# Conditioning columns loaded and multiplied later, one weight split ahead of a branch, and lower weight halves on another engine

## The chip, the cores and the metric

One core of a Trainium2 chip runs the whole program. The metric is the device time of one execution in microseconds (us). Five engines work side by side and meet at semaphores: PE (TensorE, matmuls and transposes), DVE (VectorE), ACT (ScalarE), POOL (GpSimd) and SP (SyncE), which here only issues transfers from HBM.

## The reference, cut to what matters

Two layers over 512 tokens of width 1024. Each layer has a token mixer and a mixture of experts, both between a modulation and a layer norm:

```
c_act = silu(c)
for i in range(2):
    mod = c_act @ ada_w[i] + ada_b[i]                  # [1024] @ [1024, 6144]
    sh1, sc1, g1, sh2, sc2, g2 = split(mod, 6)
    h = x * (1 + sc1) + sh1
    y = neighbourhood_mixer(h) if i == 0 else gqa_mixer(h)
    x = layer_norm(alpha * x + (1 + g1) * y)
    h = x * (1 + sc2) + sh2
    y = hierarchical_moe(h)                            # 32 experts, top 2
    x = layer_norm(alpha * x + (1 + g2) * y)
```

`gqa_mixer` projects 1024 columns of queries and 256 each of keys and values, normalises queries and keys, rotates them and attends. All is float32; a float32 product that must stay exact is made of a higher half and a lower half of each operand (`wh`, `wl` of a weight, `hTH`, `hTL` of the activations), and three of the four products are summed.

## The kernel before, in words

The program runs through these stages: the values, projections and neighbourhood attention of layer 0 (`mixer0`, to about 295 us), its output projection and norm (to 380), its experts (to 835), the norm and a conditional branch for overflowing experts (to 862), layer 1's projections (`mixer1`, 862 to 970), its attention and norm (to 1155), its experts (to 1610) and the end.

**Modulation.** `mod` has 12 columns of 512 numbers for each layer, addressed as (layer, j). A column takes two weight tiles of 1 MB (128 x 2048, names `w<-in_ada`). In `mixer0` the function `flow` writes out 32 steps n, one per head pair and query block. Each step does filling matmuls of the projections (`fill`), a `turn` (transposes of the probabilities), a `weigh` (`po`, probabilities times values) and the scores of a later step. In some steps `adap` multiplies two columns on PE: `ADAP` names the steps. An `adap` of two columns is 32 matmuls of 32 x 512 into one PSUM tile `pt` and an addition to `mod` on DVE (L699). From step 28 on there is no projection left to fill with; `aside` then calls `step`, which splits the output projection's weights `wo` into halves on ACT, DVE and POOL. After the last step come `close(7)` (normalising the last head pair, tiles `rze`), `flush` (`pt<-dacc`), the row `pw<-mod` and the output projection's sums (`pw<-w,oH` and `oL`), for which DVE makes the gate `g` (L935).

**Weights.** All weights are loaded by SP in the order of one list (`W`). A load waits until its buffer was read for the last time, and every later load of the list stands behind it. `w<-in_gu` are the first expert weights. `wq` is a ring of four 512 KB tiles for the projection weights of layer 0; it ends with them.

**Orders.** In `mixer0` the order on PE and DVE is that of the code, in the experts that on PE; elsewhere a scheduler orders each engine. SP's order is always that of the code.

**Layer 1's projections.** `mixer1` transposes the normalised rows, scales them into `hTH` (ACT, L419) and `hTL` (DVE, L427) through `hf`, and forms the keys from the weight `kv0` in the same loop over k (names `pj`). Weights are split by `split`: `wh` on ACT (L312), `wl = w - wh` on POOL or DVE (L313). Then come the values (`kv1`), `keys()` in the middle of the first queries, and four blocks of queries `q1_0` to `q1_3`, each through `proj`, `rope` (names `t`, `kk`, `sq`, `ss`) and `queries` (`hf`). `keys()` copies the keys twice into `kd` (ACT, L796) and takes the lower half by two subtractions, one on DVE (L797) and one on POOL (L798), before transposing (`pt<-c_ident,kd`).

**End of an expert stage.** The last two blocks `down` give `h`, `hx` and from them `YH` (ACT, L1414) and `YL` (DVE, L1415); eight `unit`s sum them to rows with statistics `bs` (DVE, L1434) and copies (ACT, L1435), then a norm, the branch, and layer 1.

Of the kernel before, what the change touches and what calls it, by code (L numbers as in the profile page):

```python
# [8 lines left out]
F32 = mybir.dt.float32  # L9
# [34 lines left out]
QPOST = 2  # L44
NWQ = 4
ADAV = [(0, 6), (0, 7), (0, 8), (0, 9), (1, 0), (1, 1), (1, 2)]
ADAP = {4: [(0, 4), (0, 5)], 8: [(0, 10), (0, 11)], 12: [(1, 4), (1, 5)], 15: [(1, 6), (1, 7)], 19: [(1, 8), (1, 9)],
        23: [(1, 10), (1, 11)], 26: [(1, 3)]}
STREAM = [("qk", 1, 0)] + [("qk", n, i) for i in (1, 2) for n in range(2)] + [("vq", 0)] \
    + [("qk", n, i) for i in (3, 4, 5, 6) for n in range(2)] + [("vq", 1)] + [("qk", n, 7) for n in range(2)]  # L50
RATE = (18, 15)
# [14 lines left out]
class Trunk:  # L66
    def __init__(self, ctx, tc, a, out, dbg=None):
        self.ctx, self.tc, self.nc, self.a, self.out = ctx, tc, tc.nc, a, out
        self.dbg = dbg or {}
        self.wl = []  # L70
        self.qfree = NWQ
        self.wi = 0
        self.wt = {}
        self.wpos = {}
        self.extra, self.free, self.owed, self.nh = [], [0] * NWB, 0, None

# [5 lines left out]
    def plan(self):  # L82
        a, wl = self.a, self.wl

        def add(key, ap, dst=None):
            self.wpos[key] = len(wl)
            wl.append((key, ap, dst))

        def ada(l, *js):
            for j in js:  # L90
                for h in range(2):
                    add(("ada", l, j, h), a["ada"][l, j, h])

        def direct(key, ap, dst):
            add(key, ap, dst)

        def xs(c0, c1):
            for t in range(NT):
                direct(("x", t, c0), a["x"][t][:, c0:c1], self.X[t][:, c0:c1])

        def aq(j, c):
            add(("aq", j, c), a["adaq"][j, c])

        for n, t in self.early:
            direct(n, a[n], t)
        for g in range(4):
            aq(g // 2, g % 2)
            aq(2 + g // 2, g % 2)
            if g == 0:
                for l in range(DEPTH):  # L110
                    direct(("adab", l), a["adab"][l], self.mod[l][0:NR])
                xs(0, 256)
                add(("v", 0, 0), a["wv"][0])
                add(("qk", 0, 0), a["wqk"][0, 0])
            elif g == 1:
                xs(256, 512)
            elif g == 2:
                xs(512, 1024)
                add(("v", 0, 1), a["wv"][1])
        for n, t in self.late:  # L120
            direct(n, bcast(a[n], [P, 36]) if n[:2] == "rb" else a[n], t)
        def ask(z):
            if z[0] == "ada":
                add(z, a["ada"][z[1], z[2], z[3]])
            elif z[0] == "qk":
                add(z, a["wqk"][z[1], z[2]])
            else:
                add(z, a["wvq"][z[1]])

        none = lambda *n: None  # L130
        self.flow(ask, lambda z, ahead: chunk_dry(z, ahead), none, none, none, none, lambda z, h, k: k or ask(("ada", *z, h)),
                  lambda pair: [ask(("ada", *z, h)) for z in pair for h in range(2)], none, none)
        for l in range(DEPTH):
            if l:
                for c in range(2):
                    add(("kv", c), a["wkv1"][c])
                for c in range(4):
                    add(("q1", c), a["wq1"][c])
            for h in range(2):
                for kh in range(2):  # L140
                    add(("wo", l, h, kh), a["wo"][l, h, kh])
            for h in range(2):
                for kh in range(2):
                    add(("wl", l, h, kh), None)
            for j in range(E // 2):
                for n in range(2):
                    for kh in range(2):
                        for i in range(2):
                            add(("gu", l, 2 * j + i, n, kh), a["gu"][l, 2 * j + i, n, kh])
                for fh in range(2):  # L150
                    for i in range(2):
                        add(("dn", l, 2 * j + i, fh), a["dn"][l, 2 * j + i, fh])
            self.wend = getattr(self, "wend", []) + [len(wl)]

    def flow(self, split, chunk, scores, turn, weigh, close, adav, adap, aside, end):


        todo, made, ready = list(STREAM), [0], set()
# [32 lines left out]
        for n in range(32):  # L191
            i, b = n // 4, n % 4
            if n + 1 < 32:
                if b == 3:
                    need(("qk", 1, i + 1))
                scores(n + 1)
            rate = RATE[n >= 12]
            fill(rate // 2)
            if b == 0 and i:
                close(i - 1)  # L200
            turn(n)
            if i < len(ADAV):
                for k in range(2):
                    adav(ADAV[i], b // 2, 2 * (b % 2) + k)
            aside(n)
            fill(rate - rate // 2)
            if n in ADAP:
                adap(ADAP[n])
            if n == 16:
                need(("vq", 0))  # L210
            if n == 24:
                need(("vq", 1))
            weigh(n)
            if n == 27:
                end()
# [137 lines left out]
    def ada_cols(self, pool, mod, dst, js, tag):  # L353
# [4 lines left out]
        for n, j, one in js:  # L358
            nc.vector.tensor_scalar(dst[:, n].rearrange("p (j i) -> p j i", j=2),
                                    pc[:, :, j:j + 2].rearrange("p i j -> p j i"), one, None, op0=OP.add)  # L360

    def row(self, ps, l, j):
        return self.mm(ps, bcast(self.indc[:, j:j + 1], [P, P]), self.mod[l], True, True)

# [64 lines left out]
    def mixer0(self, oT, right):  # L429
        tc = self.tc  # L430
        with tc.tile_pool(reuse_waits="tile", name="v0", bufs=1) as vp:
# [9 lines left out]
            with tc.manual_schedule(engines={mybir.EngineType.PE, mybir.EngineType.DVE}), \  # L441
                    tc.tile_pool(reuse_waits="tile", name="n0p", bufs=2, space=PSUM) as pp:
                q0 = self.values(vp, pp, hp, hH, hL, V, V6)
                with tc.tile_pool(reuse_waits="tile", name="n0", bufs=1) as pool:
                    def done():
                        ht.__exit__(None, None, None)
                        wo.extend(self.split_wo(0, right("wh", 4)))

                    self.neighbours(pool, pp, hp, hH, hL, V, V6, oT, q0, done, lambda: wo[1]())
        return wo  # L450

    def split_wo(self, l, pool):
# [133 lines left out]
    def neighbours(self, pool, pp, hp, hH, hL, V, V6, oT, q0, done, step):  # L586
# [83 lines left out]
        def close(i):  # L670
            self.scaled(pool, pp, oT[i // 4][:, i % 4, :].rearrange("p (b q) -> p b q", b=4), po[i], rz[i])
# [17 lines left out]
        def adap(pair):  # L689
# [8 lines left out]
                                tile_position=(0, r))  # L698
            nc.vector.tensor_tensor(self.mod[l], self.mod[l], ps, op=OP.add)  # L699

        def aside(n):
            i, b = n // 4, n % 4
            if b == 1 and i and i % 2 == 0:
# [6 lines left out]
            if n >= 28:  # L710
                step()

        self.flow(split, chunk, scores, turn, weigh, close, adav, adap, aside, done)
        close(7)
        self.accs, self.accl = [(j, accs.pop((l, j))) for l, j in ADAV[6:]], 1
        self.flush(pp)

    def mixer1(self, st, qS):
# [4 lines left out]
        with tc.tile_pool(reuse_waits="tile", name="m1", bufs=1) as pool, tc.tile_pool(reuse_waits="tile", name="m1p", bufs=2, space=PSUM) as pp:  # L723
# [8 lines left out]
            hL = pool.tile([P, KD, S], F32R, name="hTL")  # L732
            c1 = pool.tile([P, 2, KD], F32, name="c1")
            self.fold_cols(c1[:, 0], c1[:, 1], self.lnc[:, 0, 2], self.lnc[:, 0, 3], self.col[1][:, 0], self.col[1][:, 1])
            w = self.W(("kv", 0))
            whl = [self.split(pool, w[:, 1024 * x:1024 * x + 1024], [P, 1024], 4, (nc.vector, None)[x]) for x in range(2)]
            acc = [pp.tile([P, 4, HD], F32, name="pj", bufs=4) for t in range(NT)]
            for k in range(KD):
                self.put_hT(k, self.transp(k, pp, "pt"), hH, hL, c1[:, 0], c1[:, 1], pool, k >= KACT)
# [2 lines left out]
                for t in range(NT):  # L742
                    ts = slice(128 * t, 128 * t + 128)
                    po = acc[t].rearrange("p h d -> p (h d)")
                    self.mm(po, hH[:, k, ts], wh[:, c], k == 0, False)
                    self.mm(po, hH[:, k, ts], wl[:, c], False, False)
                    self.mm(po, hL[:, k, ts], wh[:, c], False, k == KD - 1)

            def proj(key):
                w = self.W(key)  # L750
                hl = [self.split(pool, w[:, 1024 * x:1024 * x + 1024], [P, 1024], 4) for x in range(2)]
                for t in range(NT):
                    ts = slice(128 * t, 128 * t + 128)
                    ps = pp.tile([P, 4, HD], F32, name="pj", bufs=4)
# [35 lines left out]
            def keys():  # L790
                r = root(ks.rearrange("p a b -> p (a b)"), 1.0, NT, "rs")
                for t in range(NT):
                    nc.vector.tensor_tensor(kk[t], kk[t], bcast(r[:, t, :, None], [P, 4, HD]), op=OP.mult)
                    kd = pool.tile([P, 2, 4, 2, HD], F32R, name="kd", bufs=1)
                    for d in range(2):
                        nc.scalar.activation(kd[:, 0, :, d, :], kk[t], AF.Copy)  # L796
                    nc.vector.tensor_tensor(kd[:, 1, :, 0, :], kk[t], kd[:, 0, :, 0, :].bitcast(F32), op=OP.subtract)  # L797
                    nc.gpsimd.tensor_tensor(kd[:, 1, :, 1, :], kk[t], kd[:, 0, :, 1, :].bitcast(F32), op=OP.subtract)  # L798
                    for n in range(2):
                        pt = pp.tile([P, 4, P], F32, name="pt")  # L800
                        for h in range(4):
# [477 lines left out]
    def moe(self, l, zH, zL, G2, rt, OH):  # L1279
        nc, X, tc = self.nc, self.X, self.tc  # L1280
        NQ = E // 4
        with tc.tile_pool(reuse_waits="tile", name=f"mo{l}", bufs=2) as pool, \
# [167 lines left out]
            for q in range(NQ):  # L1450
# [38 lines left out]
                    seed(range(NSEED[0]))  # L1489
                down(b, hx)  # L1490
            seed(range(NSEED[0], 8))
            for n in range(8):
                unit(n)
            self.scales(pool, rt, 0, NT)
# [142 lines left out]
```

## Time and profile before

| | |
|---|---|
| median of 3 runs | 1659.25 us (1657.05 to 1659.85) |
| the profiled execution's own time | 1659.12 us |
| its span in the trace | 1657.4 us |
| PE busy | 1569.4 us, 95% of the span |
| DVE, ACT, POOL busy | 700.5, 437.8, 162.7 us |
| moved by DMA | 493.17 MB, mean 298 GB/s |

The profiled execution took 1.7 us more than the span from its first to its last instruction. Busy shares are averages over stages of different kinds: the two expert stages keep PE and the DMA engines full at once, the stages between them keep neither full. Work is expressed in instructions of one engine; "idle before" is the time in which an engine stood still before an instruction, with the last thing that released it.

### The profile page before, as it was taken

What the parts mean: (1) busy time and instruction counts of PE and PEld (TensorE: products, weight loads), DVE (VectorE), ACT (ScalarE), POOL (GpSimd) and SP (SyncE); (2) the same over time, 40 slices, a digit from 0 to 9 for tenths busy, and PEclk for the clock granted to TensorE, in tenths of its full rate; (3) what the DMA queues carried; (4) which work ended last, traced back from release to release, by engine and by line L of the source; (5) the groups of instructions that cost most, each with busy time, mean ns of one, the idle gap of its engine ahead of it and who ended that gap; (6) DMA issues with size and microseconds to landing.
All of it is one profiled execution on the core that took longest, in us unless ns stands there. A gap on an engine that the chain in (4) does not pass through costs nothing. (4 is left out here: it accounts for less than half of the span.)

```text
span 1657.4 us, 21364 instructions
## 1 busy us (share of the span) xinstructions
PE 1569.4 (95%) x8490; PEld 903.9 (55%) x8490; DVE 700.5 (42%) x1605; ACT 437.8 (26%) x934; POOL 162.7 (10%) x99
## 2 busy tenths in 40 slices
PE   7999997989999999999989989998999999999995
PEld 5676664673544545455448866766444545445442
DVE  3434545574332322323256865666432322323235
ACT  2343335231110111111134475453111111101112
POOL 2322212010000000000013250011000000000001
PEclk9999997999999999999989999999999999999997
DMA  9586972358999999999942000035999999999971
GB/s 335 185 314 261 353 290 105 152 203 328 413 419 420 419 419 420 419 419 420 419 154 83 27 1 26 1 127 206 418 412 420 420 419 420 419 420 419 419 326 52
DMA packets 76198, 493.17 MB, mean 298 GB/s; under 512 B 9876, under 2 KB 11284, under 8 KB 18876
## 3 DMA queue, kind: packets, MB, share of 16 engines
q1 hardware_dynamic: 72636, 485.44, 72.1%
q10 hardware_dynamic: 3456, 6.29, 1.2%
q8 instruction: 69, 1.13, 0.3%
q14 instruction: 37, 0.30, 0.1%
HBM read 489.61 MB, written 2.10 MB: 297 GB/s over the span
## 5 line engine op out<-in xcount | busy, mean ns | idle before, releaser
L300 PE MATMUL gu<-w,xT 128*64 128x512 f32 x2048 | 445.1, 592 | 0.0
L300 PEld LDWEIGHTS gu<-w,xT 128*64 128x64 f32 x2048 | 146.8, 137 | 291.8 <-issue 285.5
L300 PE MATMUL pd<-w,hx 128*64 128x512 f32 x1024 | 226.8, 595 | 0.0
L1391 DVE TENSOR_TENSOR h<-h,gu 128x512 f32<-128x512 f32 x32 | 22.0, 688 | 367.5 <-PE gu L300 367.5
L300 PEld LDWEIGHTS pd<-w,hx 128*64 128x64 f32 x1024 | 70.7, 137 | 137.9 <-issue 134.3
L300 PE MATMUL gc<-OH,zH 128*128 128x256 f32 x480 | 121.8, 291 | 2.4 <-DVE OH L1276 2.4
L300 PE MATMUL gc<-OH,zL 128*128 128x256 f32 x480 | 118.9, 285 | 0.0
L300 PE MATMUL gc<-YH,OT 128*128 128x512 f32 x244 | 104.1, 427 | 1.0 <-DVE X L1358 1.0
L1358 DVE TENSOR_TENSOR X<-X,gc 128x512 f32<-128x512 f32 x128 | 87.3, 687 | 39.5 <-PE gc L300 39.5
L313 POOL TENSOR_TENSOR wl<-w,wh 128x1024 fp32r<-128x1024 f32 x19 | 46.1, 2431 | 559.5 <-DMA kk<-in_gain 494.4
L300 PEld LDWEIGHTS gc<-OH,zH 128*128 128x128 f32 x480 | 92.7, 193 | 14.7 <-issue 11.4
L300 PE MATMUL gc<-YL,OT 128*128 128x512 f32 x244 | 96.3, 395 | 0.0
L300 PEld LDWEIGHTS gc<-OH,zL 128*128 128x128 f32 x480 | 92.9, 193 | 0.0
L300 PE MATMUL pw<-w,oH 128*128 128x512 f32 x256 | 87.5, 413 | 0.4 <-DVE g L935 0.4
L1294 ACT ACTIVATE xT<-gc,A 128x256 f32<-128x256 f32 x60 | 33.8, 566 | 174.1 <-PE gc L300 174.1
L1414 ACT ACTIVATE YH<-h 128x512 fp32r<-128x512 f32 x32 | 20.2, 630 | 219.8 <-DVE h L1413 219.8
L300 PE MATMUL pj<-wh,hTH 128*128 128x256 f32 (+1 forms) x272 | 70.9, 303 | 6.7 <-ACT wh L312 2.8
L300 PE MATMUL pj<-wl,hTH 128*128 128x256 f32 (+1 forms) x272 | 68.0, 292 | 0.0
L300 PE MATMUL pj<-wh,hTL 128*128 128x256 f32 (+1 forms) x272 | 65.3, 292 | 1.4 <-DVE hTL L427 1.4
L300 PEld LDWEIGHTS gc<-YH,OT 128*128 128x128 f32 x244 | 45.8, 188 | 37.2 <-DVE X L1358 15.7
L1390 ACT ACTIVATE h<-gu 128x512 f32<-128x512 f32 x32 | 19.1, 597 | 174.3 <-PE gu L300 174.3
L1292 DVE TENSOR_SCALAR xT<-gc,A 128x256 f32<-128x256 f32 x60 | 32.5, 544 | 76.7 <-ACT xT L1294 76.3
(345 smaller groups left out, 2362.9 us busy)
## 6 DMA issues: line engine op xcount, KB each, us to landing
w<-in_gu SPq DMA_DIRECT2D x256, 1024.0 KB, 13.9
w<-in_dn SPq DMA_DIRECT2D x128, 1024.0 KB, 13.2
w<-in_ada SPq DMA_DIRECT2D x40, 1024.0 KB, 7.6
wq<-in_wqk SPq DMA_DIRECT2D x16, 512.0 KB, 3.6
w<-in_wo SPq DMA_DIRECT2D x8, 1024.0 KB, 4.8
w<-in_adaq SPq DMA_DIRECT2D x6, 1024.0 KB, 11.5
bias<-in_nab ACTq DMA_DIRECT2D x24, 256.0 KB, 4.4
w<-in_wq SPq DMA_DIRECT2D x4, 1024.0 KB, 4.8
```

The costliest lines, as they stand in the source:

```text
L300: return self.nc.tensor.matmul(out, l, r, start=start, stop=stop, **kw)
L313: (eng or nc.gpsimd).tensor_tensor(lo, src, h.bitcast(F32), op=OP.subtract)
L1292: nc.vector.tensor_scalar(xT[q][:, k, :], ps, s, b, op0=OP.mult, op1=OP.add)
L1294: nc.scalar.activation(xT[q][:, k, :], ps, AF.Identity, scale=s, bias=b)
L1358: nc.vector.tensor_tensor(X[t][:, c], X[t][:, c], ps, op=OP.add)
L1390: nc.scalar.activation(h, gu[0], AF.Silu)
L1391: nc.vector.tensor_tensor(h, h, gu[1], op=OP.mult)
L1414: nc.scalar.activation(YH[j][:, c], y, AF.Copy)
```

## The change

Three parts.

1. Layer 1's columns 6 to 11 leave `adap` at steps 15, 19 and 23. A new function `adaq` multiplies one column each after steps 28, 29, 30 and 31 and twice after `close(7)`: four tiles `wa` of 512 KB, two matmuls from each. The tiles come from a ring of four (`aq0`), which is opened when the projections of layer 0 are done and lies where their buffers were; its 24 loads stand on SP behind the four loads of `wo` and ahead of `w<-in_gu`.
2. The weight `kv0` is split at the end of layer 0's experts, ahead of the norm and the branch, into two more buffers of the weight list: two copies of 128 x 1024 on ACT and two subtractions on DVE.
3. `proj` takes the lower halves of its weights on DVE instead of POOL (ten of 128 x 1024), and `keys` makes `kd` with one ACT copy and one DVE subtraction of 128 x 512 each for a tile of tokens, instead of two copies, a DVE and a POOL subtraction of 128 x 256.

```diff
-ADAP = {4: [(0, 4), (0, 5)], 8: [(0, 10), (0, 11)], 12: [(1, 4), (1, 5)], 15: [(1, 6), (1, 7)], 19: [(1, 8), (1, 9)],
-        23: [(1, 10), (1, 11)], 26: [(1, 3)]}
+ADAP = {4: [(0, 4), (0, 5)], 8: [(0, 10), (0, 11)], 12: [(1, 4), (1, 5)], 26: [(1, 3)]}
+ADAQ = [(1, j) for j in (8, 9, 6, 7, 10, 11)]
...
             if n in ADAP:
                 adap(ADAP[n])
+            if n > 27:
+                adaq()
...
+    def ada_tiles(self):
+
+        while self.qfree and self.qa:
+            l, j, h, x = z = self.qa.pop(0)
+            t = self.qpool.tile([P, 1024], F32, name="wa", bufs=NWQ)
+            self.nc.sync.dma_start(t, self.a["ada"][l, j, h][:, 1024 * x:1024 * x + 1024])
+            self.qt.append((z, t.rearrange("p (k n) -> p k n", k=2)))
+            self.qfree -= 1
...
                         wo.extend(self.split_wo(0, right("wh", 4)))
+                        self.qpool = qp.enter_context(tc.tile_pool(reuse_waits="tile", name="aq0", bufs=1, side="right"))
+                        self.ada_tiles()
...
+        def adaq():
+            if self.qt:
+                l, j = self.qt[0][0][:2]
+                ps = pp.tile([P, F], F32, name="pt")
+                for n in range(4):
+                    _, w = self.qt.pop(0)
+                    self.qfree += 1
+                    for k in range(2):
+                        kk = 2 * n + k
+                        r = 32 * (kk % 4)
+                        self.mm(ps[r:r + 32], self.Z[:, kk, 12 - j:44 - j], w[:, k, :], kk < 4, kk > 3, tile_position=(0, r))
+                nc.vector.tensor_tensor(self.mod[l], self.mod[l], ps, op=OP.add)
+                self.ada_tiles()
...
         close(7)
+        adaq()
+        adaq()
...
-            w = self.W(("kv", 0))
-            whl = [self.split(pool, w[:, 1024 * x:1024 * x + 1024], [P, 1024], 4, (nc.vector, None)[x]) for x in range(2)]
+            whl = [[z[:, 1024 * x:1024 * x + 1024] for z in self.kv] for x in range(2)]
...
+            self.free += [0, 0]
...
-                hl = [self.split(pool, w[:, 1024 * x:1024 * x + 1024], [P, 1024], 4) for x in range(2)]
+                hl = [self.split(pool, w[:, 1024 * x:1024 * x + 1024], [P, 1024], 4, nc.vector) for x in range(2)]
...
-                    for d in range(2):
-                        nc.scalar.activation(kd[:, 0, :, d, :], kk[t], AF.Copy)
-                    nc.vector.tensor_tensor(kd[:, 1, :, 0, :], kk[t], kd[:, 0, :, 0, :].bitcast(F32), op=OP.subtract)
-                    nc.gpsimd.tensor_tensor(kd[:, 1, :, 1, :], kk[t], kd[:, 0, :, 1, :].bitcast(F32), op=OP.subtract)
+                    k2 = bcast(kk[t][:, :, None, :], [P, 4, 2, HD])
+                    nc.scalar.activation(kd[:, 0], k2, AF.Copy)
+                    nc.vector.tensor_tensor(kd[:, 1], k2, kd[:, 0].bitcast(F32), op=OP.subtract)
...
             seed(range(NSEED[0], 8))
+            if l == 0:
+                w, wH, wL = (self.W((n, 0), True) for n in ("kv", "kvH", "kvL"))
+                for x in range(2):
+                    c = slice(1024 * x, 1024 * x + 1024)
+                    nc.scalar.activation(wH[:, c], w[:, c], AF.Copy)
+                    nc.vector.tensor_tensor(wL[:, c], w[:, c], wH[:, c].bitcast(F32), op=OP.subtract)
+                self.free.append(0)
+                self.kv = wH, wL
             for n in range(8):
                 unit(n)
```

PE, end of `mixer0`, before: the last scores, the last two turns (`pr` to `pt`) with their `po`, `close(7)` (`rze`), the flush, the row and the first sums.

```order
L300 MATMUL ps<-qk_2200,qk_2129 128x256 x2
L303 MATMUL pt<-c_ident,pr 128x128 x4
L300 MATMUL po<-pts,V_94 64x128 x4
L303 MATMUL pt<-c_ident,pr 128x128 x4
L300 MATMUL po<-pts,V 64x128 x4
L303 MATMUL pt<-c_ident,rze 128x128 x4
L300 MATMUL pt<-dacc,Zo 32x512
L300 MATMUL pw<-mod_67,c_indc 128x512 x2
L300 MATMUL pw<-w_2314,oH 128x512
```

The same place of the changed kernel.

```order
L306 MATMUL ps<-qk_2122,qk_2051 128x256 x2
L309 MATMUL pt<-c_ident,pr 128x128 x4
L306 MATMUL pt<-wa,Z 32x512 x8
L306 MATMUL po<-pts,V_94 64x128 x4
L309 MATMUL pt<-c_ident,pr 128x128 x4
L306 MATMUL pt<-wa,Z 32x512 x8
L306 MATMUL po<-pts,V 64x128 x4
L309 MATMUL pt<-c_ident,rze 128x128 x4
L306 MATMUL pt<-wa,Z 32x512 x16
L306 MATMUL pt<-dacc,Zo 32x512
L306 MATMUL pw<-mod_67,c_indc 128x512 x2
L306 MATMUL pw<-w_2247,oH 128x512
```

Between each turn and the product that uses it stand eight matmuls from `wa` tiles, and sixteen stand between `rze` and the flush.

SP, loads from the last modulation tiles to the first expert weights, changed kernel.

```order
L278 DMA w_1693<-in_ada 128x2048
L278 DMA w_1799<-in_ada 128x2048
L278 DMA w_1914<-in_wo 128x2048
L278 DMA w_2042<-in_wo 128x2048
L278 DMA w_2131<-in_wo 128x2048
L278 DMA w_2160<-in_wo 128x2048
L373 DMA wa<-in_ada 128x1024 x24
L278 DMA w_3196<-in_gu 128x2048
```

The 24 `wa` loads are new between the fourth `wo` load and the first `in_gu` load; twelve loads of 1 MB have gone from further up in the queue.

DVE, from the end of layer 0's experts (`h`, `hx`, `YL`) to the first statistics of the rows, changed kernel (`w_5823<-w_5786,w_5803` is the lower half of `kv0`, its names being those of weight buffers).

```order
L1447 SCALAR_TENSOR_TENSOR h<-pd_5891,GS,G_3043 128x512
L1449 TENSOR_TENSOR YL<-h,YH 128x512
L1447 SCALAR_TENSOR_TENSOR hx<-pd_5906,GS,G_3043 128x512
L1531 TENSOR_TENSOR w_5823<-w_5786,w_5803 128x1024
L1449 TENSOR_TENSOR YL<-hx,YH 128x512
L1531 TENSOR_TENSOR w_5823<-w_5786,w_5803 128x1024
L1468 BN_STATS bs<-gc 128x6 x2
```

The two subtractions of `kv0` stand on either side of the last `YL`; in the kernel before, the same rows stand without them. Behind the branch the scheduler has this order on ACT and DVE: first the two copies `wh` and then the two subtractions `wl` of the next weight `kv1`, where before the two of `kv0` stood.

## Rows read from the trace of the kernel before

**Rows 1.** Page: busy us, share of the span and instructions by engine.

```profile
PE 1569.4 (95%) x8490; PEld 903.9 (55%) x8490; DVE 700.5 (42%) x1605; ACT 437.8 (26%) x934; POOL 162.7 (10%) x99
```

**Rows 2.** Stretches: busy of PE PEld DVE ACT POOL, granted clock, DMA share, GB/s.

```profile
257.00:295.00 38.00, 28.58 (x149) 16.20 (x148) 20.99 (x46) 19.86 (x47) 11.04 (x8) 0.69 0.28 103
380.00:835.00 455.00, 454.52 (x2307) 215.79 (x2304) 139.16 (x269) 62.04 (x119) 0.00 (x0) 1.00 1.01 417
884.30:970.00 85.70, 78.07 (x617) 73.45 (x618) 68.02 (x210) 37.01 (x91) 19.82 (x11) 0.97 0.11 38
```

**Rows 3.** PE's timeline: start us, us, operation; steps with two columns.

```profile
177.80 2.78 PE L300 MATMUL pt<-w,Z 128*32 128x512 f32 x24
...
183.01 0.66 PE L300 MATMUL po<-pts,V 128*64 128x128 f32 x8
...
205.89 3.64 PE L300 MATMUL pt<-w,Z 128*32 128x512 f32 x32
```

**Rows 4.** PE's timeline at the end of layer 0's attention.

```profile
263.01 3.64 PE L300 MATMUL pt<-w,Z 128*32 128x512 f32 x16
...
274.06 0.63 PE L303 MATMUL pt<-c_ident,rze 128*128 128x128 f32 x4 [2.27 <-DVE rze L886]
...
280.65 1.12 PE L300 MATMUL po<-pts,V 128*64 128x128 f32 x8 [1.14 <-ACT pts L658]
...
285.11 1.12 PE L300 MATMUL po<-pts,V 128*64 128x128 f32 x8 [1.14 <-ACT pts L658]
...
290.19 1.92 PE L300 MATMUL pt<-dacc,Zo 128*32 128x512 f32 x2
...
294.68 0.73 PE L300 MATMUL pw<-w,oH 128*128 128x512 f32 x2 [0.45 <-DVE g L935]
```

**Rows 5.** Busy time by stretch, as in rows 2, inside that end.

```profile
276.00:292.00 16.00, 12.75 (x58) 6.96 (x58) 10.49 (x20) 7.09 (x18) 8.35 (x6) 0.50 0.12 32
```

**Rows 6.** Transfers: output-projection loads, us to landing of 512 KB tiles, first expert loads.

```profile
L272 SPq DMA_DIRECT2D w<-in_wo x4: 328/328/328, 241.7 to 266.7; - x4
...
DMA to landing us min/median/max: 3.2/3.6/10.4
...
289.19 2.05 SPq L272 DMA_DIRECT2D w<-in_gu x4
```

**Rows 7.** DVE's timeline at the end of layer 0's experts.

```profile
849.91 0.69 DVE L1415 TENSOR_TENSOR YL<-hx,YH 128x512 fp32r<-128x512 f32 x1 [0.70 <-ACT YH L1414]
852.55 1.30 DVE L1434 BATCH_NORM_STATS2 bs<-gc 128x6 f32<-128x512 f32 x2 [1.94 <-PE gc L300]
```

**Rows 8.** Timelines of ACT and DVE behind the branch.

```profile
862.04 2.00 ACT L312 ACTIVATE wh<-w 128x1024 fp32r<-128x1024 f32 x2 [0.17 <-ACTq L1169]
...
863.14 1.23 DVE L313 TENSOR_TENSOR wl<-w,wh 128x1024 fp32r<-128x1024 f32 x1 [0.58 <-ACT wh L312]
```

**Rows 9.** Timelines of POOL, DVE and PE in layer 1's first projection.

```profile
870.68 4.70 POOL L313 TENSOR_TENSOR wl<-w,wh 128x1024 fp32r<-128x1024 f32 x2
...
873.75 2.77 DVE L427 TENSOR_TENSOR hTL<-hf,hTH 128x512 fp32r<-128x512 f32 x2 [3.64 <-ACT hf L424]
...
875.98 0.72 PE L300 MATMUL pj<-wh,hTL 128*128 128x256 f32 x4 [1.22 <-DVE hTL L427]
```

**Rows 10.** Timelines of POOL and DVE at and after the keys' sums.

```profile
885.45 2.40 POOL L313 TENSOR_TENSOR wl<-w,wh 128x1024 fp32r<-128x1024 f32 x1 [5.18 <-ACT wh L312]
...
886.01 2.12 DVE L789 TENSOR_TENSOR kk<-t,t 128x256 f32<-128x256 f32 x1
...
889.11 0.41 DVE L789 TENSOR_TENSOR kk<-t,t 128x256 f32<-128x256 f32 x1
```

**Rows 11.** Timelines of DVE and PE in the keys and the first queries.

```profile
912.52 2.22 DVE L797 TENSOR_TENSOR kd<-kk,kd 128x256 fp32r<-128x256 f32 x1
...
915.38 0.66 PE L303 MATMUL pt<-c_ident,kd 128*128 128x128 f32 x4 [1.86 <-POOL kd L798]
...
945.23 1.09 PE L303 MATMUL pt<-c_ident,hf 128*128 128x128 f32 x8 [1.10 <-DVE hf L816]
```

More of the change, by code (lines that the diff above doesn't have):

```diff
@@ L73, in __init__ @@
         self.wt = {}
+        self.qt, self.qa = [], [(l, j, h, x) for l, j in ADAQ for h in range(2) for x in range(2)]
         self.wpos = {}
@@ L131, in plan @@
         self.flow(ask, lambda z, ahead: chunk_dry(z, ahead), none, none, none, none, lambda z, h, k: k or ask(("ada", *z, h)),
-                  lambda pair: [ask(("ada", *z, h)) for z in pair for h in range(2)], none, none)
+                  lambda pair: [ask(("ada", *z, h)) for z in pair for h in range(2)], none, none, none)
         for l in range(DEPTH):
@@ L136, in plan @@
                     add(("kv", c), a["wkv1"][c])
+                    if c == 0:
+                        add(("kvH", c), None)
+                        add(("kvL", c), None)
                 for c in range(4):
@@ L153, in plan, with flow @@
             self.wend = getattr(self, "wend", []) + [len(wl)]
-    def flow(self, split, chunk, scores, turn, weigh, close, adav, adap, aside, end):
+    def flow(self, split, chunk, scores, turn, weigh, close, adav, adap, adaq, aside, end):
         todo, made, ready = list(STREAM), [0], set()
@@ L447, in done @@
                         wo.extend(self.split_wo(0, right("wh", 4)))
-                    self.neighbours(pool, pp, hp, hH, hL, V, V6, oT, q0, done, lambda: wo[1]())
+                        self.qpool = qp.enter_context(tc.tile_pool(reuse_waits="tile", name="aq0", bufs=1, side="right"))
+                        self.ada_tiles()
+                    with ExitStack() as qp:
+                        self.neighbours(pool, pp, hp, hH, hL, V, V6, oT, q0, done, lambda: wo[1]())
         return wo
@@ L711, in aside @@
                 step()
-        self.flow(split, chunk, scores, turn, weigh, close, adav, adap, aside, done)
+        self.flow(split, chunk, scores, turn, weigh, close, adav, adap, adaq, aside, done)
         close(7)
+        adaq()
+        adaq()
+        assert not self.qa and not self.qt
         self.accs, self.accl = [(j, accs.pop((l, j))) for l, j in ADAV[6:]], 1
```

## The prediction

> **What bounds the kernel now.** I read the page first: PE is busy 95% of the span, DVE and POOL far less [rows 1]. That average says nothing of a single stage, so I next cut the span into stretches [rows 2]. From 380 to 835 PE is busy 454.52 of 455.00 us at a granted clock of 1.00 while the DMA engines are busy throughout at 417 GB/s: nothing that this change touches lies there, and a load that comes a few us later ahead of it is of no account. The change works in two stretches of another kind. From 257 to 295 PE is busy 28.58 of 38 us at a mean clock of 0.69, and the DMA engines move 103 GB/s: this is the tail of layer 0's attention, where PE waits and runs at half clock. From 884.3 to 970 PE is busy 78.07 of 85.70 us and DVE 68.02: PE leads, but DVE is close behind it. Then I read PE's timeline at each place for the waits that end last [rows 3, 4, 9, 11], and the timelines of the engines named there.
>
> **Part 1, what it removes.** The three steps with two columns end at PE, which does nothing else meanwhile. The first takes from 177.80 to 183.01, 5.2 us, the others 3.6 us each, the busy time of their 32 matmuls less the overlap at its end [rows 3]. Sum: 12.4 us, and everything behind step 26 comes that much earlier. The two columns of step 26 end at 263.01 + 3.64 = 266.65 now [rows 4], at 254.3 then.
>
> **Part 1, what it adds.** The last loads of `wo` wait for step 26's tiles: the last of four is issued at 266.7 [rows 6], as that step ends. Two of them (2.1 MB, for the step's tiles free their buffers at its end) would go at 254.3, and behind them 24 tiles of 0.524 MB, 12.6 MB. At the 417 GB/s of the expert stage [rows 2] these 14.7 MB take 35.2 us. A tile lands 3.2 us after its issue at the least [rows 6], of which 0.524 MB at 417 GB/s are 1.3, so 1.9 us are to be added once. The last `wa` tile lands at 254.3 + 35.2 + 1.9 = 291.4 at the earliest. PE alone would be there sooner: its work from 266.65 to the flush at 290.19 is 23.5 us [rows 4], so the flush could start at 277.8, and six times eight matmuls more are, at the half clock at which 16 took 3.64 [rows 4], 10.9 us, of which some lies in the 1.14 us that PE waits for `pts` in each step [rows 4]: about 286. So the tail turns from PE's into the transfers'.
>
> From the last tile to the first sums: one read of two matmuls, 0.5 us, and then flush, row and gate, 294.68 - 290.19 = 4.5 us at half clock [rows 4]; some 4 us of it are matmuls (1.92 for the flush, the row about as long), which halve at full clock, so 2.5. The first sums come at 291.4 + 0.5 + 2.5 = 294.4 if the transfers never pause and the clock is full, 296.4 at half clock. They pause when PE reads late, since each tile is loaded into a slot that PE must have read: a round of four tiles takes 5.0 us by the transfers, and for PE at half clock a step of 285.11 - 280.65 = 4.46 us less the 1.14 us of wait, plus 1.8 us of reading [rows 4], 5.1 to 6.3 us. For three rounds that is between nothing and 3.9 us more. I take half clock for about half of the tail: 296.0, against 294.68 before, **+1.3 us**, with bounds of -0.3 and +5.6. So the 12.4 us are given back to the transfers, to within this rest. The expert weights, queued behind the tiles, start near 291 instead of 289.19 [rows 6] and are needed at 380 only.
>
> The Trainium skill ("DMA: Bandwidth & Descriptors", Specifications) gives a core's limit towards HBM as about 358 GB/s; by it, an estimate, the 14.7 MB would take 41 us and the tail would end some 6 us later. The trace disagrees: 417 GB/s over 455 us [rows 2].
>
> **Part 2.** Two subtractions of 1.23 us [rows 8] join DVE at the end of the experts. The first lies between `hx` and its `YL`. DVE stood idle 0.70 us there [rows 7], so `YL` starts 0.5 us later, and PE's last sums with it. The second ends 849.91 + 0.53 + 0.69 + 1.23 = 852.4, ahead of the statistics at 852.55 [rows 7]. ACT's two copies (2.00 us [rows 8]) lie between the two `YH`, where it has nothing to do. Cost: +0.5 us (0 to 1.2, if the copies come late). The gain behind the branch is nothing by itself: ACT's first work there is then `wh` of `kv1`, as long as that of `kv0` before, and the first `hTH` comes behind it as before.
>
> **Part 3 and the rest of layer 1.** DVE instructions beside a running POOL subtraction are long: two `hTL` took 2.77 us during POOL's `wl` (2 x 0.69 by the `YL` of the same shape), and PE waited 1.22 us for them [rows 7, 9]; `kk` took 2.12 us, and 0.41 three us later without POOL [rows 10]. With the lower halves on DVE these cases go. Gains on PE's path: 1.2 us at 875.98; 0.4 of the 1.7 us of `kk`, which has slack; and of the 1.86 us that PE waited for POOL's half of `kd` [rows 11] 1.5, since DVE's own subtraction must still come. Together 3.1 us (at most 1.7 + 1.7 + 1.9 = 5.3, at least nothing).
>
> The price is DVE's load. Ten lower halves of 1.23 us are 12.3 us, and four larger `kd` 4 x (0.69 - 0.41) = 1.1; the long cases return at least 1.7 (`kk`) and 1.8 (`kd`, 2.22 [rows 11]). That is up to 9.9 us more on 68.02 [rows 2], 78 of about 83 us, 94%. Most of it falls into DVE's gaps. Where DVE is already late, at 945.23 with 1.10 us [rows 11], a lower half stands ahead of `hf` now and another in the chain before it: I take +0.7 us of their 2.5, with bounds of nothing and 4.9, four lower halves in full on the path. Part 3: -3.1 + 0.7 = **-2.4 us** (-5.3 to +4.9).
>
> **The sum.** 1659.12 (the profiled execution's own time, 0.13 below the median) + 1.3 + 0.5 - 2.4 = **1658.5 us**. A measurement of this kernel can tell about 0.2%, 3.3 us, from no change, so this is no change that can be measured.
>
> **The rivals.**
>
> A, faster: the transfers run without a pause behind a PE at full clock, and POOL's stalls cost more than I count. The mean clock of 0.69 from 257 to 295 against 0.50 from 276 to 292 [rows 2, 5] means that it was higher before 276, and PE had then just stood 2.27 us ahead of `rze` [rows 4]; `adaq` fills gaps. Against it: PE would have less work per round (about 3.5 us of 5.0) than in the stretch from 276 to 292, where it was busy 12.75 of 16 us and yet at 0.50 [rows 5]. The time: -0.3 for the tail, 0 for part 2, -5.3 + 0.7 in layer 1: 1654.2; with 3.6 of the 5.3 it is 1655.9, the edge of what can be told.
>
> B, slower, by the ring: PE stays at half clock and hides none of its waits behind `adaq`, so each of five rounds is 4.46 + 1.8 = 6.3 us, and the first ends when its tiles land, 254.3 + (2.1 + 2.1) MB / 417 GB/s + 1.9 = 266.3. Last read at 266.3 + 31.5 = 297.8, first sums at 302.3, +7.6: 1659.12 + 7.6 + 0.5 - 2.4 = 1664.8. For it the 0.50 of [rows 5]; against it that transfers of later tiles need not wait for the whole round. It decides from a round of about 5.9 us on.
>
> C, slower, by DVE: the lower halves stand in front of what PE waits for, four times 1.23 us, and little is gained: 1659.12 + 1.3 + 0.5 - 1.2 + 4.9 = 1664.6. For it the 94%; against it that in the rows read the one wait of 1.10 us for `hf` shows DVE as late [rows 11].
>
> D, slower, by the transfers' rate: at 358 GB/s instead of 417 the tail ends 5.8 us later, 1664.3. The rows speak against it.
>
> E: part 1 does nothing because the removed steps were filling time in which PE would have waited for ACT. Then one of the three steps, say, returns nothing, the tail starts 4 us later and all of it shifts: 1662.5. Against it, no other work stands in those steps' rows but PE's [rows 3].
>
> **How the numbers follow.** Forecast 0.46, A 0.31, B 0.11, C 0.07, D 0.02, E 0.03. Faster by over 0.2%: A, 0.31. Slower: B to E, 0.23 (E lies on the edge). Same: 0.46. The range for 8 in 10 reaches from 1651 (A with all of its bounds and a little of the second waits that POOL causes and I have not followed) to 1664.5, just short of B's and C's centres. The forecast's own range is 1656 to 1662.
>
> **What would show it.** Step 26's columns end at about 254.3, and the stretch before has no new waits (else E). PE's timeline has six groups of eight matmuls from `wa`, the later ones waiting for DMA by 1 to 3 us each, 5.0 us apart, and the first sums between 294 and 298. The granted clock from 264 to 292 decides between A and B. `YL` of `hx` starts about 0.5 us later against its `hx`. In layer 1 no `hTL`, `kk` or `kd` takes over 1 us, the wait for POOL's `kd` is gone, and the stretch that was 862 to 970 lasts 105 to 106 us instead of 108. A wait of PE for DVE of over 1.5 us, more than once between 910 and 960, would be C. The prediction is wrong if the tail's rounds are not those of the transfers, or if DVE's gaps do not hold the lower halves.

## The result

The changed kernel took 1668.94 us in the median of five runs (1662.86 to 1673.07), the kernel before 1658.24 (1656.80 to 1659.85): a ratio of 1.0065, with a 95% interval of 1.0049 to 1.0082. Two repeats (`again` and `early_ring` below, whose edit moved nothing) gave 1.0078 (1.0065 to 1.0091) and 1.0073 (1.0056 to 1.0090). The kernel became slower, beyond the range of the prediction. Its five runs lie 10 us apart; in the repeats they lie 3.8 and 5.3 us apart, so that width did not come back. One execution of `four_columns` below took 3146 us and is left out of its ratio.

The profiled execution is the fastest of the five: 1662.86 us, span 1661.1. The page of the changed kernel, the lines that answer to [rows 1]:

```profile
span 1661.1 us, 21384 instructions
PE 1570.8 (95%) x8490; PEld 899.9 (54%) x8490; DVE 703.8 (42%) x1619; ACT 438.0 (26%) x930; POOL 131.5 (8%) x84
```

Busy times have hardly changed; POOL has lost 31 us. What changed is where PE waits. Its timeline in the tail of layer 0's attention, changed kernel (start, us, operation, idle before):

```profile
249.68 3.55 PE L306 MATMUL pt<-w,Z 128*32 128x512 f32 x16
...
260.19 1.09 PE L309 MATMUL pt<-c_ident,rze 128*128 128x128 f32 x4 [2.27 <-DVE rze L920]
...
265.08 1.05 PE L306 MATMUL pt<-wa,Z 128*32 128x512 f32 x4 [0.24 <-DMA wa<-in_ada]
...
272.34 1.05 PE L306 MATMUL pt<-wa,Z 128*32 128x512 f32 x4 [0.20 <-DMA wa<-in_ada]
...
278.65 1.05 PE L306 MATMUL pt<-wa,Z 128*32 128x512 f32 x4 [0.23 <-DMA wa<-in_ada]
...
286.22 1.05 PE L306 MATMUL pt<-wa,Z 128*32 128x512 f32 x4 [0.20 <-DMA wa<-in_ada]
...
293.04 1.05 PE L306 MATMUL pt<-wa,Z 128*32 128x512 f32 x4 [0.22 <-DMA wa<-in_ada]
...
300.14 0.62 PE L306 MATMUL pt<-wa,Z 128*32 128x512 f32 x2 [0.21 <-DMA wa<-in_ada]
...
300.60 0.60 PE L306 MATMUL pt<-wa,Z 128*32 128x512 f32 x2
...
305.07 0.71 PE L306 MATMUL pw<-w,oH 128*128 128x512 f32 x2 [1.96 <-DVE g L969]
```

Step 26 ends at 253.2 instead of 266.65 (254.3 was forecast). Then each of the six groups ends with a tile that has only just landed: the rows at 265.08, 272.34 and so on are the last tiles of the groups, 6.3 to 7.6 us apart, 7.0 on average. The first sums start at 305.07 against 294.68 [rows 4]: 10.4 us later. One profile of each kernel tells this only to some 3 us: three kernels below whose tail is that of the kernel before have their first sums at 291.69, 292.89 and 293.01. Busy time by stretch, and SP's loads, of the same kernel (columns as in [rows 2]; the transfers' three numbers as in [rows 6]):

```profile
265.00:300.00 35.00, 24.73 (x136) 6.69 (x136) 9.84 (x22) 6.97 (x18) 6.54 (x6) 1.00 0.91 313
...
253.68 40.77 SPq L373 DMA_DIRECT2D wa<-in_ada  x24
294.51 2.15 SPq L278 DMA_DIRECT2D w<-in_gu  x4
...
DMA to landing us min/median/max: 3.8/5.8/9.9
```

The granted clock is 1.00 here, and PE is busy 24.73 of 35 us: the transfers set the pace, and they move 313 GB/s, not 417. After the first sums little happens until layer 1. From them to the first `gu` 80.7 us pass (82.1 before), the last `YL` of layer 0 starts 9.4 us later than before, and the first `pj` 9.2 us. In layer 1's projections 4.3 us come back: from the first `pj` to the first `ps` of attention there were 107.07 us, and there are 102.75:

```profile
864.77:971.84 107.07, 97.09 (x741) 90.22 (x741) 77.78 (x220) 51.95 (x114) 33.51 (x20) 0.95 0.14 51
```

```profile
873.96:976.71 102.75, 96.91 (x740) 89.72 (x741) 79.92 (x229) 49.79 (x108) 4.79 (x5) 0.93 0.20 73
```

The first of these rows is of the kernel before, the second of the changed one. PE's work is the same, 97 us; its idle time fell from 10.0 to 5.8. The end of the span comes 3.7 us later in this fast run: 10.4 less 1.4, then 4.3 less, and about 1 us less in the rest.

### The profile page after: what moved, and what is told of

The parts are those of the page before. It is cut to its first block, busy times and chain, and to the rows that moved or that the text cites. A ratio compares the mean times of both kernels' runs of the same rounds, so it can differ in the third digit from the quotient of the medians.

```text
span 1661.1 us, 21384 instructions
## 1 busy us (share of the span) xinstructions
PE 1570.8 (95%) x8490; PEld 899.9 (54%) x8490; DVE 703.8 (42%) x1619; ACT 438.0 (26%) x930; POOL 131.5 (8%) x84
## 5 line engine op out<-in xcount | busy, mean ns | idle before, releaser
L306 PE MATMUL gc<-YH,OT 128*128 128x512 f32 x244 | 104.1, 427 | 1.1 <-DVE X L1392 1.1
L306 PE MATMUL pj<-wh,hTH 128*128 128x256 f32 (+1 forms) x240 | 60.5, 296 | 4.6 <-ACT wh L318 2.8
L309 PE MATMUL pt<-c_ident,pr 128*128 128x128 f32 x384 | 58.5, 280 | 2.1 <-ACT pr L896 1.9
L1433 ACT ACTIVATE hx<-tp 128x512 f32<-128x512 f32 x32 | 19.0, 594 | 151.6 <-PE tp L309 151.6
L306 PE MATMUL pj<-wl,hTH 128*128 128x256 f32 (+1 forms) x240 | 58.7, 289 | 0.0
```

Source lines behind the costliest of these rows:

```text
L306: return self.nc.tensor.matmul(out, l, r, start=start, stop=stop, **kw)
L309: self.nc.tensor.transpose(out, in_, self.ident)
L1433: nc.scalar.activation(hx, pt, AF.Copy)
```

## The experiments

Theory T: the loss is the tail's, where 24 loads through a ring of four small tiles carry less than the 417 GB/s on which the forecast rests. Rivals: the loss comes from layer 1 or the expert stages (R), or from PE's own work and order in the tail (P).

**again**: the changed kernel without an edit.

> The changed kernel as it is, once more, for a second profile: its five runs lay between 1662.9 and 1673.1 us while the kernel before stays within 3 us, and the one profiled was the fastest. Theory T (the tail of layer 0's attention is paced by the 24 small transfers): a median near 1668 and, where the profiled run is slower than 1662.9, the added time between 250 and 305 us, in longer rounds of the six groups from wa (7.0 us on average in the first profile), with the later stages as long as before. Rival R (what varies is elsewhere, the expert stages at 409 instead of 417 GB/s): the first sums again near 305 and the stretch from the first sums to the end longer.

Measured: 1672.05 us (1669.76 to 1673.55), ratio 1.0078. The profiled run has a span of 1671.0, 9.9 us more than the first profile, and 7.9 of them lie in the tail. PE's first sums, loads, and stretches of this run:

```profile
312.97 0.70 PE L306 MATMUL pw<-w,oH 128*128 128x512 f32 x2 [1.35 <-DVE g L969]
...
DMA to landing us min/median/max: 3.8/6.0/11.3
```

```profile
275.00:280.00 5.00, 4.64 (x22) 1.19 (x20) 0.69 (x1) 0.00 (x0) 0.00 (x0) 0.66 0.75 241
...
295.00:300.00 5.00, 2.21 (x12) 0.29 (x8) 1.15 (x2) 0.00 (x0) 0.00 (x0) 1.00 0.71 224
```

The first sums come at 312.97, 7.9 us later than in the first profile, and from there to the first `gu` of layer 1 it is 855.7 us (853.8 there). The groups end 8.1 us apart on average. The two stretches shown are among those in which the transfers paused: 241 GB/s at a granted clock of 0.66, and 224 GB/s at 1.00, so a fallen clock is not needed for a pause. Most of the added time lies where T has it, and only some 2 us behind the first sums, where R has it.

**no_part1**: parts 2 and 3 alone.

```diff
-ADAP = {4: ..., 12: [(1, 4), (1, 5)], 26: [(1, 3)]}
-ADAQ = [(1, j) for j in (8, 9, 6, 7, 10, 11)]
+ADAP = {4: ..., 12: [(1, 4), (1, 5)], 15: [(1, 6), (1, 7)], 19: [(1, 8), (1, 9)],
+        23: [(1, 10), (1, 11)], 26: [(1, 3)]}
+ADAQ = []
```

> Part 1 undone, parts 2 and 3 kept. T: the tail is that of the kernel before (first sums near 294.7), and what parts 2 and 3 gained in the first profile, 4.3 us between the first pj behind the branch and the first ps of attention, stays: 1654 to 1655 us, ratio 0.997, and runs as close together as before's. R (the loss lies in part 2 or 3, or the gain there is a gift of part 1): 1658 us or more.

Measured: 1653.15 us (1650.13 to 1655.56), ratio 0.9966 (0.9954 to 0.9978); first sums at 292.89. The gain of parts 2 and 3 stays without part 1, and the loss goes. Of the 5.3 us by which this profiled run is shorter than that of the kernel before, 1.8 lie ahead of the first sums, in a tail that the edit leaves as it was, so they are no gain of parts 2 and 3.

**only_part1**: parts 2 and 3 undone (`kv0` split after the branch, `proj` on POOL, `kd` in two copies and two subtractions, all as before).

> Part 1 alone, parts 2 and 3 undone. T: the first sums near 305, later stages as before, 1659.1 + 9 = 1668 in a run like the first profile's and 1672 in the median, ratio 1.006 to 1.009. R: near 1658.

Measured: 1674.92 us (1673.45 to 1678.24), ratio 1.0096 (1.0082 to 1.0111); first sums at 312.76. More than expected, and the whole loss.

**big_tiles**: the 2 MB ring as two tiles of 1 MB.

```diff
+NRING = 2
...
-            t = self.qpool.tile([P, 1024], F32, name="wa", bufs=NWQ)
-            self.nc.sync.dma_start(t, self.a["ada"][l, j, h][:, 1024 * x:1024 * x + 1024])
+            t = self.qpool.tile([P, 2048], F32, name="wa", bufs=NRING)
+            self.nc.sync.dma_start(t, self.a["ada"][l, j, h])
...
```

> Changed kernel with the same ring of 2 MB cut into two tiles of 1 MB (8 KB to a partition) instead of four of 512 KB (4 KB to a partition). If the size of the pieces sets the pace (355 GB/s for a fully busy set of DMA engines in the tail, 418 with 1 MB loads in the expert stage), the busy DMA engines carry 418 GB/s and, at the same share of 0.91, a round falls from 7.0 to 5.5 us: first sums near 298, 1656 to 1661 us. If the ring's slots set it (a load cannot start until PE has read its slot), two coarser slots make it worse: rounds of 8 us or more, first sums near 311 or later.

Measured: 1667.17 us (1666.25 to 1668.18), ratio 1.0051 (1.0036 to 1.0065); first sums at 308.12. Neither outcome: larger pieces did not bring the 298, and two coarse slots did not bring 311. The transfers still pause: DMA share 0.64 to 0.92 in the stretches of 5 us between 265 and 300. The same 2 MB in four tiles had its first sums at 305.07, 307.99, 312.76 and 312.97 in its four profiles, and 308.12 lies among them: how the 2 MB are cut made no difference that can be told.

**no_loads**: the first four tiles are kept and read again.

```diff
+            if len(self.kept) < NWQ:
+                t = self.qpool.tile([P, 1024], F32, name=f"wa{len(self.kept)}")
+                self.nc.sync.dma_start(t, ...)
+                self.kept.append(t)
+            t = self.kept[2 * h + x]
```

> Changed kernel with only the first four wa tiles loaded and kept: the later columns multiply them again, so 20 of 24 loads and all waits for them are gone, while PE's, DVE's and ACT's work stays (layer 1's columns 6, 7 and 9 to 11 become wrong, and the output with them). T: PE alone needs far less than the transfers; first sums near 287 (step 26 ends at 253 to 254, before's 28 us from there to the first sums, and 5 us of matmuls at full clock), no wait of PE for wa but the first, and 1645 us: 1653 of the kernel without part 1, less 6 to 8. Rival P (the 48 matmuls between the turns and the order forced on PE cost the time): first sums at 300 or later and 1660 us or more.

Measured: 1647.82 us (1645.92 to 1648.18), ratio 0.9944 (0.9927 to 0.9960). PE's timeline has the second group, the last two groups and the first sums here, with no wait for `wa` (a matmul of the program stands as two in these rows, so a group of eight is x16):

```profile
268.65 1.92 PE L307 MATMUL pt<-wa,Z 128*32 128x512 f32 x16
...
279.66 3.64 PE L307 MATMUL pt<-wa,Z 128*32 128x512 f32 x32
...
287.46 0.70 PE L307 MATMUL pw<-w,oH 128*128 128x512 f32 x2 [1.41 <-DVE g L973]
```

First sums at 287.46, forecast 287: P falls. PE's 48 further matmuls cost less than what was removed ahead of them: the first sums come 5.4 us earlier than in no_part1. The time of this kernel's later stages depends on what the wrong columns make of the routing, so only its tail is used.

**ring_of_8**: as the changed kernel, eight tiles of 512 KB (`bufs=NRING`, `NRING = 8`).

> Changed kernel with a ring of eight 512 KB tiles instead of four, same loads. If slots that PE has not read yet stop the transfers (DMA engines busy 0.83 to 0.91 of the time from 254 to 300), the engines now stay busy, and only the rate of the small pieces is left, 355 GB/s: 14.7 MB in 41.4 us from 254.8, first sums near 302 in every run, 1657 to 1661 us, runs within 4 us of each other. If the ring does not matter and the rate does: as before, 1668 to 1672.

Measured: 1656.91 us (1655.52 to 1659.37), ratio 0.9997 (0.9987 to 1.0008). Its last read, first sums and loads:

```profile
292.87 0.60 PE L307 MATMUL pt<-wa,Z 128*32 128x512 f32 x2
...
297.34 0.71 PE L307 MATMUL pw<-w,oH 128*128 128x512 f32 x2 [1.96 <-DVE g L971]
...
DMA to landing us min/median/max: 8.2/9.1/13.9
```

PE's waits for `wa`, changed kernel and then ring_of_8 (us in total, times, longest), and the stretch:

```profile
PE pt L306 <- DMA wa<-in_ada: 9.6, 13, 1.9
...
PE pt L307 <- DMA wa<-in_ada: 2.3, 10, 0.3
...
265.00:292.00 27.00, 23.83 (x138) 6.67 (x136) 9.92 (x22) 5.86 (x16) 6.31 (x6) 1.00 1.03 411
```

The same loads in the same pieces now move 411 GB/s at the same granted clock of 1.00, and PE waits 2.3 us for `wa` in all. So the bytes that the ring holds set the pace. My figure of 355 GB/s for small pieces in the expectations falls with it: I had divided the rate by a busy share, and the share misled.

**big_ring_of_4**: four tiles of 1 MB, otherwise as big_tiles (`NRING = 4`).

> Changed kernel with a ring of four tiles of 1 MB, so both twice the slots and twice the piece. If the pace is slots times pieces, this is the tail that I had forecast: 14.7 MB at 418 GB/s in 35.2 us from 254.8, last tile 292, first sums 296 to 297, 1653 to 1655 us. If only one of the two matters, it lies with ring_of_8 or with big_tiles (308, 1667).

Measured: 1656.44 us (1654.84 to 1657.30), ratio 0.9991 (0.9982 to 1.0001); first sums at 297.37. Stretch:

```profile
265.00:292.00 27.00, 18.48 (x144) 6.26 (x145) 11.21 (x22) 5.28 (x15) 7.22 (x6) 0.93 1.01 418
```

418 GB/s, and the last tile's read starts at 291.2. The first sums are those of ring_of_8: twice the piece adds nothing that can be told once the ring holds 4 MB.

**early_ring**: the call that opens the ring and issues its first loads, put ahead of the call that asks for `wo`.

> Changed kernel with the first four wa loads issued ahead of the four wo loads instead of behind them; ring and sizes as they are. In the changed kernel the DMA engines stand idle from 246 to 254 (rate 0) since the last wo loads wait for step 26 and the wa loads stand behind them. T: the first 2.1 MB move into that idle time, and the whole tail comes about 5 us earlier, 1663 to 1667 us. Rival: wo comes later by as much, step 28's splits wait for it, and nothing is gained: 1668 to 1672.

Measured: 1668.70 us (1665.52 to 1670.80), ratio 1.0073 (1.0056 to 1.0090); first sums at 307.99. The edit moved nothing: on SP the four `wo` loads still stand first, since they are issued by an earlier call that runs ahead in the list of weights, and the DMA engines moved nothing from 246 to 250. The question is not answered; the run counts as one more repeat.

**only_part2** and **only_part3**: one part alone.

> Part 2 alone (kv0 split ahead of the branch). Without part 1 the two other parts together took 5.2 us off the median. From the profile of the changed kernel part 2 cost 0.15 us up to the first pj, and POOL's subtraction in the first projection loop is gone: between no change and 1 us less, 1657 to 1658.5 us, ratio 0.9993 to 1.0002. If it is worth more than 2 us, the parts share their gain in a way that I have not seen.

Measured: 1659.57 us (1655.47 to 1662.43), ratio 1.0011 (1.0001 to 1.0022): slightly slower, by an interval that barely leaves out no change, and outside what I expected.

> Part 3 alone (lower halves and kd on DVE). By the waits of PE that went (POOL's kd 2.1 us, hf 0.9 us less, pr 0.9 us): 1654 to 1655 us, ratio 0.9975 to 0.9985, and no long hTL, kk or kd beside POOL in the queries. If part 3 only pays with part 2, near 1658.

Measured: 1653.18 us (1651.51 to 1655.65), ratio 0.9976 (0.9967 to 0.9985). Part 3 carries the gain alone. Together the two parts gave 0.9966, an interval that overlaps this one: that they add up is not shown.

**four_columns** and **two_columns**: parts 2 and 3, a ring of four tiles of 1 MB, and fewer columns in it.

```diff
+ADAP = {..., 23: [(1, 10), (1, 11)], 26: [(1, 3)]}                          # four_columns
+ADAQ = [(1, j) for j in (8, 9, 6, 7)]
...
+ADAP = {..., 19: [(1, 8), (1, 9)], 23: [(1, 10), (1, 11)], 26: [(1, 3)]}    # two_columns
+ADAQ = [(1, j) for j in (6, 7)]
```

> Parts 2 and 3, and part 1 with four columns instead of six (steps 15 and 19; step 23 keeps its two) from a ring of four tiles of 1 MB. T: 10.5 MB at 418 GB/s from 256.5 end near 284, PE without waits would have its first sums near 289, so the transfers no longer end last: first sums 289 to 291, 1649 to 1651 us, ratio 0.994 to 0.9955, and better than the kernel without part 1 (1653.2). If the transfers still set the tail, first sums at 293 or later and no gain against that kernel.

> As four_columns, with only step 15's two columns moved. T: PE sets the tail (transfers end near 278), so of the 5 us removed ahead some 2 are spent in the tail on two groups of eight matmuls: first sums near 291, 1650 to 1652 us, about 1 us more than four_columns.

Measured: four_columns 1651.89 us, ratio 0.9972 (0.9960 to 0.9984), first sums at 291.75; two_columns 1653.76 us, ratio 0.9982 (0.9973 to 0.9991), first sums at 292.43. For both I had expected 1 to 4 us less. The transfers no longer end last in two_columns (1.0 us of waits for `wa`), and cost 4.9 us of waits in four_columns. No version with part 1 beats no_part1 by more than the intervals: moving these columns gives nothing that can be told here.

## Why the prediction was wrong

**The step that failed** is the size of "Part 1, what it adds", put at +1.3 us with bounds of -0.3 and +5.6. It measured +10.4 us in the first profile and +18.3 in the second; by the medians of no_part1 and the changed kernel it is about 16. The mechanism was right: "the tail turns from PE's into the transfers'", and the 12.4 us are given back there. Wrong was the sentence "a round of four tiles takes 5.0 us by the transfers". That is the time of 2.1 MB at 417 GB/s, which needs transfers that never pause. But a slot's cycle is its load plus its read: the loads of the changed kernel landed 5.8 us after their issue in the median, and a read took 1.05 us, together 6.9 us, beside the round of 7.0 that PE's timeline shows. Four tiles of 0.524 MB in 7.0 us are 300 GB/s. I had added once, for the whole tail, the 1.9 us that a landing takes beyond its bytes; in every round, 5.0 + 1.9 = 6.9 us would have fitted what was measured, though no run takes that term by itself. What shows that the ring set the pace is ring_of_8, where nothing but the number of slots changed. There the landing rose to 9.1 us, and 4.2 MB in 9.1 + 1.05 us are 413 GB/s, beside the measured 411; that is no second proof, since a ring that is kept full gives this landing by arithmetic, at whatever rate it runs. With that ring the forecast of the tail holds to within 1.6 us: last tile read at 293.5 (291.9 forecast), first sums at 297.3 (296.0 forecast, 294.4 to 296.4 without pauses).

**The end of the tail** was mis-sized too. From the last read to the first sums I had put 2.5 us at full clock. At a granted clock of 1.00 it took 3.9 us, in the changed kernel (301.2 to 305.07) and in ring_of_8 (293.5 to 297.3): PE stood 1.96 us for the gate `g`, ahead of which DVE had the addition of the last column and four more instructions to do.

**The removal** was right: step 26 ends at 253.2 and 254.4 in the two profiles of the changed kernel, and between 264.7 and 266.7 in the kernel before and the three others profiled that keep the early columns, 10 to 13 us earlier beside the 12.4 forecast. So E falls.

**Right by luck** was that "PE alone would be there sooner". The sum for it took 3.64 us as the half-clock price of 16 matmuls. But the rows count each matmul of the program twice: step 26 has one column, not two, and its x16 are eight matmuls (an `adap` of two columns is 16, not 32). At half clock the six groups would cost 6 x 3.64 = 21.8 us, not 10.9, and 277.8 + 21.8 is past the 291.4 of the transfers, by more than the waits of 1.14 us take off. In no_loads PE ran at a granted clock of 1.00 from 268.6 on, eight matmuls took 1.92 us, and the flush came at 283.1 beside the 286 forecast.

**Part 2**, +0.5. DVE's timeline at the end of layer 0's experts, changed kernel:

```profile
857.51 0.75 DVE L1447 SCALAR_TENSOR_TENSOR hx<-pd,GS,G 128x512 f32<-128x512 f32 x1 [1.29 <-PE pd L306]
858.18 1.22 DVE L1531 TENSOR_TENSOR w<-w,w 128x1024 fp32r<-128x1024 f32 x1
859.31 0.68 DVE L1449 TENSOR_TENSOR YL<-hx,YH 128x512 fp32r<-128x512 f32 x1
859.91 1.22 DVE L1531 TENSOR_TENSOR w<-w,w 128x1024 fp32r<-128x1024 f32 x1
861.59 1.30 DVE L1468 BATCH_NORM_STATS2 bs<-gc 128x6 f32<-128x512 f32 x2 [0.46 <-PE gc L306]
```

The first subtraction fills the gap ahead of `YL` [rows 7]: from `hx` to `YL` 1.80 us pass instead of 1.44 (848.47 to 849.91 before), 0.4 us more, and the second is done ahead of the statistics, both as forecast. Alone the part measured 1.0011, some 1.8 us. Its profile is 2.8 us longer than before in layer 1's projections (109.8 us from the first `pj` to the first `ps`); but only_part1, which has neither part 2 nor part 3, takes 109.0 there, so the runs do not show that part 2 costs this.

**Part 3**, -2.4: -4.0 us alone by its ratio. The mechanism was right, and the size nearly: the profile of only_part3 has 104.1 us from the first `pj` to the first `ps`, 3.0 less than before, and its tail, which part 3 does not touch, is 3.0 us shorter as well. PE's waits from 835 to 975, kernel before and then changed kernel (us in total, times, longest):

```profile
PE pt L303 <- DVE hf L816: 2.7, 3, 1.5
PE pt L303 <- POOL kd L798: 2.1, 2, 1.9
PE pj L300 <- DVE t L775: 1.7, 2, 1.4
...
PE pj L300 <- DVE hTL L427: 1.4, 2, 1.2
```

```profile
PE pt L309 <- DVE hf L850: 1.8, 3, 1.5
PE pj L306 <- DVE t L810: 1.4, 1, 1.4
PE pt L306 <- DVE rtu L298: 1.1, 1, 1.1
PE pj L306 <- DVE hTL L442: 0.6, 3, 0.3
```

The wait for POOL's `kd` is gone whole (I counted 1.5 of 1.9), and the waits for `hf`, which I let grow by 0.7, shrank by 0.9: DVE's added instructions fell into its gaps, and C falls. One sign that I named was wrong: "no `hTL`" over 1 us. Two took 2.37 us in the changed kernel, while POOL made the rotation tables:

```profile
877.67 2.16 POOL L765 TENSOR_TENSOR rt<-rt,kk 128x256 f32<-128x256 f32 x2 [0.66 <-DMA kk<-in_gain]
...
878.01 2.37 DVE L442 TENSOR_TENSOR hTL<-hf,hTH 128x512 fp32r<-128x512 f32 x2
```

**The rivals.** B named the right place, the ring, but the wrong cause: PE at half clock in rounds of 6.3 us. In the first profile the clock was 1.00 from 265 to 300 and a round took 7.0 all the same. With eight matmuls at 3.64 us instead of 1.8, B's rounds would have been 8.1 us and its time 1673.8 us, near the repeats; that would have been luck, since the second profile, with rounds of 8.1 us, has the clock at 0.95 or more from 265 to 300 but for 0.66 between 275 and 280. What the second profile adds to the first, and which comes first there, the pause or the fall of the clock, stays open, and so do the 10 us between the first five runs. D's 358 GB/s was nearer to the rate seen (313) than my 417, for a cause that ring_of_8 excludes: the same pieces moved 411 there. The Trainium skill's limit of 358 GB/s towards HBM ("DMA: Bandwidth & Descriptors", Specifications) is thus no explanation either; the runs show 411 and 418.

## What to carry to other kernels

The bandwidth of a stage that keeps many loads queued does not hold for a ring: reckon bytes of the ring over (landing under load + read), with the full rate as the ceiling, and compare that with the rate that the work needs; 2 MB gave 300 to 313 GB/s here, 4 MB all of it. The landing under load is the hard part: with the median of 3.6 us that the kernel before shows for such tiles [rows 6] the same sum gives 451 GB/s and no loss, and it was 5.8 us here. A ring with room to spare is the safer answer. Work that is moved from a full engine into a gap must bring its data through the gap too, and what was hidden behind a long stage becomes its pace. A change in several parts is worth taking apart: one part here hid a gain of 0.24% in another.

## What the runs showed of the hardware that was not expected

The busy share of the DMA engines is not in proportion to what they move: 0.91 went with 313 GB/s in the changed kernel, 1.03 with 411 in ring_of_8, for the same loads. Pieces of 4 KB to a partition cost little against 8 KB, 411 beside 418 GB/s in one profile each. A tile that came alone took PE 1.05 us (x4, changed kernel), one of four that were there already 0.48 (x16 in 1.92, no_loads), both at a granted clock of 1.00. And DVE instructions were stretched not only beside POOL's subtraction of 128 x 1024 but also beside its products of 128 x 256: 2.37 us for two `hTL`, each 0.69 where POOL stood still.
